# Moving one SBUF tile, and all tiles below it, down by 32 bytes in a two-layer encoder trunk

## The chip, the cores and the metric

The kernel runs on one core of a Trainium2 chip. The metric is the device time of one execution in microseconds (us); less is better. The core has a matrix engine (TensorE, PE in the profile, with its weight loads listed as PEld), VectorE (DVE), ScalarE (ACT), GpSimd (POOL), a queue engine (SyncE, SP) that issues most transfers, and 16 DMA engines. SBUF is the on-chip memory: 128 partitions, and a tile has the same byte address in each of them. PSUM holds the sums of TensorE.

## The reference

Two layers work on 512 tokens of 1024 features. In each layer:

```
proj = h @ w_in[l]                       # 1024 -> 1536, cut into q, k, v of two head groups
oa = global attention, ob = windowed attention, both normed per head
h = layer_norm(ALPHA * h + concat(oa, ob) @ w_o[l])
q = (h @ wq)                             # 8 heads x 2 halves x 128
pick, per token and head, the 16 best of 128 x 128 experts; g = softmax of their scores
a = gelu(u[e] . h) for each picked expert e;   w = g * a
h = layer_norm(ALPHA * h + sum_e w[e] * v[e])
```

The expert tables `u` and `v` have 16384 rows of 1024 float32 each per layer. This last part takes most of the time.

## The kernel before

**Two ways to the experts.** The 512 tokens are four chunks of 128. Chunk 0 (`gat`) gathers the rows of its picked experts by indirect DMA and works on VectorE. Chunks 1 to 3 (`dense`, `ND` = 384 tokens) multiply with all experts on TensorE, 128 experts (a block) at a time, and the gates that are zero drop what isn't wanted. There are `NB` = 128 blocks per layer.

**Splitting float32.** Every large product is made of three products of reduced operands (`F32R`): an operand x is cast to a high part on ScalarE, and VectorE subtracts to get the low part; then hi·hi, hi·lo and lo·hi are summed in PSUM.

**First expert product** (`acts`, lines 850 to 852). For a block, `ut` (the turned expert rows) is loaded, split into `uh` and `ul`, and for each of 8 slices of the features TensorE runs

```
pe.matmul(b[:, :ND], uh[:, k, :], xTh[:, k, :], ...)
pe.matmul(b[:, :ND], uh[:, k, :], xTl[:, k, :], ...)
pe.matmul(b[:, :ND], ul[:, k, :], xTh[:, k, :], ...)
```

The first operand is stationary (its 128 columns are loaded as weights), the second is the moving one (384 columns stream through). So a group of this product is 24 matmuls, and there are 256 groups. `xTh` and `xTl` are the two halves of the tile `xT`, the turned tokens.

**Second expert product** (`combine`, lines 1044 to 1046). `vt` is split into `vh` and `vl`, the weighted activations `w` into `wh` and `wl`, and for three chunks and two halves of the features the three products go into six PSUM banks. `wh` and `wl` are stationary, `vh` and `vl` moving with 512 columns. A group is 18 matmuls; there are 256 groups.

**Order on TensorE.** In each layer 24 groups of the first product (`LEAD`) are made ahead, in part between the small products of `spread` that build the gates (lines 917 and 918); then 104 times a group of the first product stands before a group of the second; and 24 groups of the second come last. In those last ones (`turn`) the operands take turns: tiles of the pool `ep`, then pieces of the tile `xT`, then the places of `uh`, `ul` and `ge`.

**Where tiles lie.** Pools open on the left side (addresses from below) or on the right (from the top down). On the right `xq` opens first; it has one place of 24576 bytes per partition, which `hTl` (low part of the tokens for the projections), then `oTp` (attention output of the first two chunks), then `xT` use in turn. Below it lie `kp` and `tp` (ranking of the keys), later `sp` (`o12`, `ah`, `al`, half of the `stg`) and then `ep` (`vh`, `vl`, `w`, `wh`, `wl`, the accumulators of the gather). All other operands of the products (`hTh`, `whi`, `wlo`, `wqh`, `wql`, `woh`, `wol`, `uh`, `ul`, the `ge` places, and `ut`, `vt`, `gg`) lie on the left.

Other products of this kind with 256 moving columns: the projections (lines 280 to 282; `hTh`/`hTl` stationary, the split weights moving), the queries of the key ranking (lines 547 to 549; split weights stationary, `xT` moving) and the attention output (lines 448 to 450; `oTp` stationary, split weights moving).

Of the kernel before, what the change touches and what calls it, by code (L numbers as in the profile page):

```python
# [9 lines left out]
F32R = mybir.dt.float32r  # L10
# [8 lines left out]
P = 128  # L19
D = 1024  # L20
KD = D // P
S = 512
# [14 lines left out]
GB = 4  # L37
LEAD = 24
REST = 3
NTAIL = 6  # L40
NCAND = [TK // (a + 1) for a in range(TK)]
COFF = [sum(NCAND[:a]) for a in range(TK)]
# [4 lines left out]
def encoder_kernel(ctx: ExitStack, tc: tile.TileContext, x, ln_in_g, ln_in_b, w_in, qn_g, kn_g, sink,  # L47
# [9 lines left out]
    ND = len(dense) * P  # L57
# [8 lines left out]
    def sbuf(name, bufs=1, side="left"):  # L66
        return tc.alloc_tile_pool(name=name, bufs=bufs, side=side, reuse_waits="tile")
# [55 lines left out]
    def transpose_rows(src, dst, nm, lo=None, gain=None, halves=(0, 1)):  # L123

        for q in halves:
            qs = slice(q * 4, (q + 1) * 4)
            b = acc_bank(nm)
            for i in range(4):
                k = q * 4 + i
                pe.transpose(b[:, i * P:(i + 1) * P], src[:, k * P:(k + 1) * P], ident)  # L130
            bv = b.rearrange("p (k t) -> p k t", k=4)
            if gain is not None:
                v.tensor_tensor(out=dst[:, qs, :], in0=bv, in1=bc(gain[:, qs, None], [P, 4, P]), op=MUL)
            else:
                act.copy(dst[:, qs, :], bv)
            if lo is not None:
                v.tensor_tensor(out=lo[:, qs, :], in0=bv, in1=dst[:, qs, :].bitcast(F32), op=SUB)
# [62 lines left out]
    for l in range(L):  # L200
        xq = sbuf(f"xq{l}", side="right")
# [55 lines left out]
        order = dense + gat  # L257
        pj = sbuf(f"pj{l}", bufs=2)
        hTh = pj.tile([P, KD, S], F32R, name="hTh", bufs=1)
        hTl = xq.tile([P, 2 * KD * ND], F32R, tag="x", name="hTl")[:, :KD * S].rearrange("p (k t) -> p k t", k=KD)  # L260
        def load_split(src, nm, w=None):

            w = load_w(src, nm) if w is None else w
            r = []
            for i in range(2):
                x_ = w[:, i * D:(i + 1) * D]
                hi = pj.tile([P, 4, 256], F32R, tag="whi", name="whi", bufs=4)
                lo = pj.tile([P, 4, 256], F32R, tag="wlo", name="wlo", bufs=4)
                act.copy(hi.rearrange("p k n -> p (k n)"), x_)
                v.tensor_tensor(out=lo.rearrange("p k n -> p (k n)"), in0=x_,  # L270
                                in1=hi.rearrange("p k n -> p (k n)").bitcast(F32), op=SUB)
                r.append((hi, lo))
            return r
# [196 lines left out]
        def flip_out(c, half):  # L470
            x_ = ao.tile([P, KD, P], F32, tag="oT", name="oT", bufs=1) if half == 0 else st[c]["oTx"]
            st[c]["oTx"] = x_
            if half == 0:
                st[c]["oT"] = x_, None
                if c in order[:2]:
                    if c == order[0]:
                        t = xq.tile([P, 2 * KD * ND], F32R, tag="x", name="oTp")
                        st["pair"] = t[:, :KD * S].rearrange("p (i k t) -> p i k t", i=2, k=KD)
                    ci = order.index(c)
                    st[c]["oT"] = tuple(st["pair"][:, i, :, ci * P:(ci + 1) * P] for i in range(2))  # L480
            transpose_rows(st[c]["o"].rearrange("p n d -> p (n d)"), x_, f"tr_o{c}", gain=gn, halves=(half,))
            hi, lo = st[c]["oT"]
            if lo is not None:
                qs = slice(half * 4, half * 4 + 4)
                act.copy(hi[:, qs, :], x_[:, qs, :])
                v.tensor_tensor(out=lo[:, qs, :], in0=x_[:, qs, :], in1=hi[:, qs, :].bitcast(F32), op=SUB)
# [190 lines left out]
        def flip_x(g, ci, half):  # L677
            if (ci, half) == (0, 0):
                if g == 0:
                    t = xq.tile([P, 2, KD, ND], F32R, tag="x", name="xT")  # L680
                    xTs["d"] = t[:, 0], t[:, 1]
                    xTs[g] = t[:, 0, :, :2 * P], t[:, 1, :, :2 * P]
                else:
                    pl, tag = (ac, "q") if g == 1 else (pt, "xT")
                    xTs[g] = pl.tile([P, KD, P], F32, tag=tag, name=f"xT{g}", bufs=1), None
            c = groups[g][ci]
            hi, lo = (t if t is None else t[:, :, ci * P:(ci + 1) * P] for t in xTs[g])
            transpose_rows(h[:, c, :], hi, f"tr_x{c}", lo=lo, halves=(half,))
            if (g, half) == (1, 1):
                hi_, lo_ = (t[:, :, 2 * P:] for t in xTs["d"])  # L690
                act.copy(hi_, hi)
                v.tensor_tensor(out=lo_, in0=hi, in1=hi_.bitcast(F32), op=SUB)
# [36 lines left out]
        for i in range(n + 3):  # L729
# [12 lines left out]
            if 0 <= i - 3 < n:  # L742
                c, hd = hs_[i - 3]
                values(c, hd, pTs.pop(i - 3))
                if hd == 15:
                    finish(c)
                    if c != order[3]:
                        at(i + 4, flip_out, c, 0)
                        at(i + 5, flip_out, c, 1)
                    if c == order[1]:  # L750
                        for j in range(4):
                            at(i + 6 + j, mix2, order[:2], j)
                        for u in range(2):
                            for half in range(2):
                                at(i + 9, norm_pair, order[u], half)
                        for u in range(2):
                            for half in range(2):
                                at(i + 12 + 2 * u + half, flip_x, 0, u, half)
                        at(i + 16, lambda: first.append(start(0)))
                        for u in range(16, 32):  # L760
                            if u % 4:
                                at(i + u, lambda: next(first[0]))
                    if c == order[2]:
                        for j in range(4):
                            at(i + 6 + j, mix2, [c], j)
                        at(i + 9, layer_norm, c, g_1, b_1)
                        for half in range(2):
                            at(i + 13 + half, flip_x, 1, 0, half)
# [8 lines left out]
        for half in range(2):  # L777
            flip_out(last, half)
# [8 lines left out]
        for half in range(2):  # L787
            flip_x(2, 0, half)
# [148 lines left out]
        for i, _ in enumerate(spread()):  # L937
            if i % 2 == 0 and len(gel) < LEAD - REST:
                next(am)
# [112 lines left out]
        with tc.manual_schedule(engines={mybir.EngineType.DVE}):  # L1052
            for g2 in range(NB // 2):
# [8 lines left out]
                for bi in range(2):  # L1062
# [4 lines left out]
                    if turn == 1:  # L1067
                        t = xTs["d"][blk // 3 % 2].rearrange("p k n -> p (k n)")
# [16 lines left out]
                    v.tensor_tensor(out=wl, in0=wf, in1=wh.bitcast(F32), op=SUB)  # L1085
                    if blk < NB - NTAIL:
                        for c in dense:
# [91 lines left out]
```

## Time and profile before

| | us |
|---|---|
| median of 3 runs (3043.37 to 3045.31) | 3043.95 |
| the profiled execution, its own time | 3047.03 |
| its span, first to last instruction | 3045.3 |
| TensorE busy | 2974.0 |
| VectorE busy | 2447.4 |
| ScalarE busy | 1318.1 |

The profiled execution is 3.1 us over the median, and 1.7 us of its time lie outside the span. Busy time of TensorE is the union of its matmuls; each is drawn from the start of its stream to the end of its drain, so neighbours overlap, and the distance from one start to the next is what a matmul takes of the span. The granted TensorE clock was 0.994 of full speed over the span.

### The profile page before, as it was taken

How to read it: one execution, taken by the hardware profiler on the slowest of the kernel's cores; microseconds unless marked ns; L12 is line 12 of the kernel's file. 1: busy time of each engine (PE TensorE's matmuls, PEld its weight loads, DVE VectorE, ACT ScalarE, POOL GpSimd, SP SyncE). 2: the span in 40 equal slices, each digit the busy share in tenths (PEclk: the TensorE clock that was granted, in tenths of full speed). 3: DMA queues.
4: the chain of work that ended last, by engine and by line, in shares of the span. 5: the costliest groups of instructions: out<-in, count | busy, mean ns of one | idle time of the engine just before them, and what ended most of it. 6: DMA issues, size and time to landing. Idle time of an engine off the chain costs nothing.

```text
span 3045.3 us, 48000 instructions
## 1 busy us (share of the span) xinstructions
PE 2974.0 (98%) x18034; PEld 2734.8 (90%) x18034; DVE 2447.4 (80%) x5084; ACT 1318.1 (43%) x2642; POOL 749.8 (25%) x524
## 2 busy tenths in 40 slices
PE   7999999999999999999999999999999999999998
PEld 7999899899999999998798998998999999999987
DVE  7777999778887887877777779997787788778877
ACT  4665167433333333333347641774333333333332
POOL 0000000014443455554000000000244444555530
PEclk9999999999999999999999999999999999999999
DMA  5014766669889989988420247666689998999882
GB/s 197 26 63 143 256 244 267 215 210 331 316 324 326 330 309 331 323 322 301 159 97 15 72 153 272 249 255 215 224 316 332 326 328 312 330 323 332 313 297 90
DMA packets 262233, 749.47 MB, mean 246 GB/s; under 512 B 19952, under 2 KB 130288, under 8 KB 231792
## 3 DMA queue, kind: packets, MB, share of 16 engines
q1 hardware_dynamic: 188272, 477.94, 43.8%
q0 software_dynamic: 73728, 268.47, 24.6%
q8 instruction: 141, 2.31, 0.3%
q14 instruction: 92, 0.75, 0.1%
HBM read 691.81 MB, written 54.53 MB: 245 GB/s over the span
## 4 chain that ended last, share of the span: by engine, by line
PE 72%; DVE 12%; issue 6%; DMA 5%; POOL 3%; ACT 2%; DVEq 0%; POOLq 0%; ACTq 0%
PE ps_a L850 10%; PE ps_a L852 10%; PE ps_a L851 10%; PE ff L1046 9%; PE ff L1045 9%; PE ff L1044 9%; DMA gt<-in_dram,idx 5%; POOL gt L1001 3%; PE ps_o L415 2%; PE ps_g L918 1%; PE ps_g L917 1%; PE ps_pt L401 1%; PE ps_s L377 1%; DVE ix L571 1%; PE ps_q L282 1%
## 5 line engine op out<-in xcount | busy, mean ns | idle before, releaser
L1001 POOL DMA_INDIRECT gt<-in_dram,idx x512 | 740.4, 1446 | 2014.8 <-DMA ut<-in_dram 1218.1
L850 PE MATMUL ps_a<-xT,uh 128*128 128x384 f32 x2048 | 697.1, 340 | 0.3
L852 PE MATMUL ps_a<-xT,ul 128*128 128x384 f32 x2048 | 695.9, 340 | 0.0
L851 PE MATMUL ps_a<-xT,uh 128*128 128x384 f32 x2048 | 694.9, 339 | 0.0
L1046 PE MATMUL ff<-vh,wl 128*128 128x512 f32 x1440 | 566.3, 393 | 0.0
L1045 PE MATMUL ff<-vl,wh 128*128 128x512 f32 x1440 | 564.3, 392 | 0.0
L1044 PE MATMUL ff<-vh,wh 128*128 128x512 f32 x1440 | 560.5, 389 | 2.1 <-ACT wh L1084 2.1
L1077 ACT CAST vh<-vt 128x1024 fp32r<-128x1024 f32 x240 | 251.7, 1050 | 561.3 <-PE ff L1046 290.0
L1078 DVE TENSOR_TENSOR vl<-vt,vh 128x1024 fp32r<-128x1024 f32 x240 | 293.8, 1224 | 132.7 <-ACT vh L1077 132.3
L851 PEld LDWEIGHTS ps_a<-xT,uh 128*128 128x128 f32 x2048 | 385.0, 188 | 9.6
L850 PEld LDWEIGHTS ps_a<-xT,uh 128*128 128x128 f32 x2048 | 385.0, 188 | 8.7 <-ACT ge L854 0.6
L852 PEld LDWEIGHTS ps_a<-xT,ul 128*128 128x128 f32 x2048 | 384.9, 188 | 0.0
L1018 DVE SCALAR_TENSOR_TENSOR gacc<-gt,gw,gacc 128x1024 f32<-128x1024 f32 x252 | 313.2, 1281 | 46.3 <-DMA gt<-in_dram,idx 45.9
L847 ACT CAST uh<-ut 128x1024 fp32r<-128x1024 f32 x256 | 269.8, 1054 | 178.7 <-PE ps_a L851 168.8
L1007 DVE CUSTOM_DVE_ANT_0 junk<-gt,h 128x1024 bf16<-128x1024 f32 x256 | 313.1, 1223 | 34.8 <-DMA gt<-in_dram,idx 30.1
L848 DVE TENSOR_TENSOR ul<-ut,uh 128x1024 fp32r<-128x1024 f32 x256 | 312.3, 1220 | 21.1 <-ACT uh L847 14.4
L1084 ACT CAST wh<-w 128x384 fp32r<-128x384 f32 x240 | 123.3, 514 | 468.3 <-DVE w L1081 468.1
L1046 PEld LDWEIGHTS ff<-vh,wl 128*128 128x128 f32 x1440 | 270.2, 188 | 57.2
L1044 PEld LDWEIGHTS ff<-vh,wh 128*128 128x128 f32 x1440 | 270.6, 188 | 54.7 <-ACT wh L1084 2.8
L1045 PEld LDWEIGHTS ff<-vl,wh 128*128 128x128 f32 x1440 | 270.2, 188 | 52.9
L1085 DVE TENSOR_TENSOR wl<-w,wh 128x384 fp32r<-128x384 f32 x240 | 134.0, 558 | 154.1 <-ACT wh L1084 154.1
L1081 DVE SCALAR_TENSOR_TENSOR w<-gg,ge 128x384 f32<-128x384 f32 x256 | 141.8, 554 | 6.2 <-DMA gg<-G 6.2
(278 smaller groups left out, 4630.1 us busy)
## 6 DMA issues: line engine op xcount, KB each, us to landing
ut<-in_dram SPq DMA_DIRECT2D x128, 1024.0 KB, 8.9
vt<-in_dram SPq DMA_DIRECT2D x128, 1024.0 KB, 7.6
w_pq<-in_dram SPq DMA_DIRECT2D x48, 1024.0 KB, 5.1
gg<-G SPq DMA_DIRECT2D x62, 768.0 KB, 15.0
G<-stg SPq DMA_DIRECT2D x24, 1920.0 KB, 6.3
w_o<-in_dram SPq DMA_DIRECT2D x24, 1024.0 KB, 4.9
w_q<-in_dram SPq DMA_DIRECT2D x8, 1024.0 KB, 5.4
gt<-in_dram,idx POOLq DMA_INDIRECT x512, 7.6
```

The source lines that it names most:

```text
L847: act.copy(uh.rearrange(ff), us)
L848: v.tensor_tensor(out=ul.rearrange(ff), in0=us, in1=uh.rearrange(ff).bitcast(F32), op=SUB)
L850: pe.matmul(b[:, :ND], uh[:, k, :], xTh[:, k, :], start=k == 0, stop=False)
L851: pe.matmul(b[:, :ND], uh[:, k, :], xTl[:, k, :], start=False, stop=False)
L852: pe.matmul(b[:, :ND], ul[:, k, :], xTh[:, k, :], start=False, stop=k == KD - 1)
L1001: pool.indirect_dma_start(out=t, out_offset=None, in_=src, in_offset=bass.IndirectOffsetOnAxis(ap=idx[:, j:j + 1], axis=0))
L1007: v.tensor_tensor_reduce(out=jk, in0=t, in1=h[:, c, :], op0=MUL, op1=ADD, scale=1.0, scalar=0.0, accum_out=a_[:, j:j + 1])
L1018: v.scalar_tensor_tensor(acc[j % 2], t, w_[:, j:j + 1], acc[j % 2], op0=MUL, op1=ADD)
L1044: pe.matmul(b, wh[:, cs], vh[:, ns], start=blk == 0, stop=False)
L1045: pe.matmul(b, wh[:, cs], vl[:, ns], start=False, stop=False)
L1046: pe.matmul(b, wl[:, cs], vh[:, ns], start=False, stop=blk == NB - 1)
L1078: v.tensor_tensor(out=vl, in0=vt[:, bi, :], in1=vh.bitcast(F32), op=SUB)
```

## The change

A constant `PAD` = 8 is added, and the three tiles that use the place in `xq` are asked for with 8 more float32 elements. The elements added are not used. The place grows from 24576 to 24608 bytes per partition, and as it hangs from the top of SBUF, it begins 32 bytes lower, and so does each tile of the right side below it. Nothing on the left moves.

```diff
+PAD = 8
...
-        hTl = xq.tile([P, 2 * KD * ND], F32R, tag="x", name="hTl")[:, :KD * S].rearrange("p (k t) -> p k t", k=KD)
+        hTl = xq.tile([P, 2 * KD * ND + PAD], F32R, tag="x", name="hTl")[:, :KD * S].rearrange("p (k t) -> p k t", k=KD)
...
-                        t = xq.tile([P, 2 * KD * ND], F32R, tag="x", name="oTp")
+                        t = xq.tile([P, 2 * KD * ND + PAD], F32R, tag="x", name="oTp")
...
-                    t = xq.tile([P, 2, KD, ND], F32R, tag="x", name="xT")
+                    t = xq.tile([P, 2 * KD * ND + PAD], F32R, tag="x", name="xT")[:, :2 * KD * ND].rearrange("p (i k t) -> p i k t", i=2, k=KD)
```

Addresses of the built programs, as the remainder modulo 256 (the slices of an operand that the matmuls take begin at multiples of 512 bytes in its tile, and share its remainder):

| operands | before | after |
|---|---|---|
| `uh`, `ul`, `ge` places, `hTh`, `whi`, `wlo`, `wqh`, `wql`, `woh`, `wol`, `qT`, `khh`, `kll`, `ut`, `vt`, `gg` | 192 | 192 |
| `xT`, `oTp`, `hTl` | 224 | 192 |
| `vh`, `vl`, `wh`, `wl`, `w` in `ep` | 224 | 192 |
| `keys`, `pq`, `psc`, `o12`, `ah`, `al`, the `stg` in `sp` | 224 | 192 |

In the built programs the instructions of every engine and every queue are the same in kind, shape, names and order; their line numbers are one higher, as the new constant takes a line.

## Rows read from the trace of the kernel before

**Rows 1.** The page's first part: busy us (share of the span) xinstructions.

```profile
PE 2974.0 (98%) x18034; PEld 2734.8 (90%) x18034; DVE 2447.4 (80%) x5084; ACT 1318.1 (43%) x2642; POOL 749.8 (25%) x524
```

**Rows 2.** Busy time in two stretches of 150 us, one of each layer's expert products.

```profile
core 0: us, PE busy (x) PEld busy (x) DVE busy (x) ACT busy (x) POOL busy (x), PEclk, DMA share, GB/s
...
900.00:1050.00 150.00, 150.00 (x754) 136.49 (x753) 120.70 (x172) 53.54 (x72) 63.21 (x50) 1.00 0.91 323
...
2550.00:2700.00 150.00, 150.00 (x754) 136.63 (x753) 120.56 (x129) 54.18 (x73) 76.36 (x50) 1.00 0.90 322
```

**Rows 3.** Waits of ScalarE: us in total, times, longest us.

```profile
ACT vh L1077 <- PE ff L1046: 290.0, 110, 2.9
```

**Rows 4.** Groups of TensorE by shape: busy us, mean ns of one.

```profile
L850 PE MATMUL ps_a<-xT,uh 128*128 128x384 f32 x2048 | 697.1, 340 | 0.3
L852 PE MATMUL ps_a<-xT,ul 128*128 128x384 f32 x2048 | 695.9, 340 | 0.0
L851 PE MATMUL ps_a<-xT,uh 128*128 128x384 f32 x2048 | 694.9, 339 | 0.0
L1046 PE MATMUL ff<-vh,wl 128*128 128x512 f32 x1440 | 566.3, 393 | 0.0
L1045 PE MATMUL ff<-vl,wh 128*128 128x512 f32 x1440 | 564.3, 392 | 0.0
L1044 PE MATMUL ff<-vh,wh 128*128 128x512 f32 x1440 | 560.5, 389 | 2.1 <-ACT wh L1084 2.1
...
L377 PE MATMUL ps_s<-kll,qT 128*128 128x384 f32 x32 | 10.8, 338 | 0.0
```

**Rows 5.** Timeline, TensorE, one group of each expert product: start us, us.

```profile
1001.21 0.39 PE L1044 MATMUL ff<-vh,wh 128*128 128x512 f32 x1
...
1003.29 0.39 PE L1044 MATMUL ff<-vh,wh 128*128 128x512 f32 x1
...
1005.11 0.40 PE L1046 MATMUL ff<-vh,wl 128*128 128x512 f32 x1
1005.34 0.34 PE L850 MATMUL ps_a<-xT,uh 128*128 128x384 f32 x1
...
1009.40 0.34 PE L852 MATMUL ps_a<-xT,ul 128*128 128x384 f32 x1
1009.58 0.39 PE L1044 MATMUL ff<-vh,wh 128*128 128x512 f32 x1
```

**Rows 6.** Timeline, TensorE, a late group whose operands lie in the tile xT.

```profile
1428.08 0.39 PE L1044 MATMUL ff<-xT 128*128 128x512 f32 x1
...
1431.93 0.40 PE L1046 MATMUL ff<-xT 128*128 128x512 f32 x1
1432.17 0.39 PE L1044 MATMUL ff<-vh,wh 128*128 128x512 f32 x1
```

**Rows 7.** Timeline, TensorE, two early groups of the first expert product, among spread's.

```profile
503.87 0.33 PE L851 MATMUL ps_a<-xT,uh 128*128 128x384 f32 x1
...
507.68 0.34 PE L852 MATMUL ps_a<-xT,ul 128*128 128x384 f32 x1
...
509.94 0.34 PE L851 MATMUL ps_a<-xT,uh 128*128 128x384 f32 x1
...
513.83 0.34 PE L852 MATMUL ps_a<-xT,ul 128*128 128x384 f32 x1
```

**Rows 8.** Timeline, TensorE, products of 256 columns: projections, then queries of the keys.

```profile
86.09 0.28 PE L280 MATMUL ps_q<-whi,hTh 128*128 128x256 f32 x1
...
91.77 0.28 PE L280 MATMUL ps_q<-whi,hTh 128*128 128x256 f32 x1
...
1812.92 0.28 PE L547 MATMUL ps_pq<-xT,wqh 128*128 128x256 f32 x1
...
1815.02 0.28 PE L547 MATMUL ps_pq<-xT,wqh 128*128 128x256 f32 x1
```

**Rows 9.** Groups of VectorE: the same subtraction into left tiles and into right ones.

```profile
L848 DVE TENSOR_TENSOR ul<-ut,uh 128x1024 fp32r<-128x1024 f32 x256 | 312.3, 1220 | 21.1 <-ACT uh L847 14.4 <-PE ps_g L918 6.7
L1078 DVE TENSOR_TENSOR vl<-vt,vh 128x1024 fp32r<-128x1024 f32 x240 | 293.8, 1224 | 132.7 <-ACT vh L1077 132.3
```

## The prediction, made before the changed kernel ran

> **What bounds the kernel.** The page's busy times come first: TensorE is busy for 2974.0 of 3045.3 us, VectorE for four fifths [rows 1]. A share over the span says little, so the next view is the busy time by stretches. In both layers' expert products TensorE is busy for 150.00 of 150.00 us at a granted clock of 1.00 (of 2.4 GHz), VectorE for 121 us, and the DMA engines are at 0.91 and 0.90 [rows 2]. Who waits for whom agrees: ScalarE stood 290.0 us before the cast into `vh` until TensorE let go of the buffer [rows 3]. So in this stretch, which is over half the span, every nanosecond between two matmul starts is in the end time, and the reader has to look at the distance of starts, not at the drawn durations, which overlap.
>
> The timeline gives that distance. A group of the second product takes 1001.21 to 1005.34, 4.13 us for 18 matmuls of 512 columns; one of the first product 1005.34 to 1009.58, 4.24 us for 24 matmuls of 384 [rows 5]. At 2.4 GHz, 512 columns are 213.3 ns and 384 are 160.0 ns. The means are 229.4 and 176.7 ns. So each matmul loses 16 to 17 ns to something, some 8% of the stretch, and only that can answer to a change of addresses.
>
> **Does an offset matter at all?** While one matmul streams, the weights of the next are read from the same memory. Call a step *equal* where the moving operand and the next weights have the same remainder modulo 256, else *unequal*. Before, the second product is equal inside (224 and 224, or 192 and 192 in its last turns), the first is unequal (`xT` 224, `uh` and `ul` 192). Three readings speak for an influence.
>
> First, inside a group of the second product the distance isn't constant. The first nine take 1001.21 to 1003.29, 231 ns each; the next eight 1003.29 to 1005.11, 227.5 ns each [rows 5]. It settles. In the late group with operands in `xT` it is settled from the start: 1428.08 to 1431.93, 17 steps of 226.5 ns [rows 6]. The last step of that group, the only one to weights at 192, is 0.24 us [rows 6]; and the step from the second to the first product, unequal too, is 0.23 (1005.11 to 1005.34) [rows 5]. So an unequal step appears to throw the pattern out, and it takes nine equal steps to settle again.
>
> Second, the first product, unequal at every step, has two patterns. Two early groups 6 us apart: 503.87 to 507.68 is 22 steps of 173.2 ns, 509.94 to 513.83 is 22 steps of 176.8 ns [rows 7]; the groups of the long stretch are of the second kind (176.7). 173.2 is the settled 226.5 of the second product less 53.3 for 128 columns. A loss of 13.2 ns is thus what settled matmuls show at either width.
>
> Third, the one equal product of 384 columns, the window scores, has a mean duration of 338 ns where the first expert product has 340, 340 and 339 [rows 4]; its 32 instances stand alone between transposes, so they show a size and not a settled state.
>
> **The change, part by part.** Instructions, their order, waits and transfers stay. What changes:
>
> *First expert product, now equal.* I take it that the settled loss holds at 384 columns too: 24 steps of 173.2 instead of 176.7 ns, 84 ns a group. 208 groups stand between groups of the second product: 17.5 us. Of the 48 early ones half are already settled by the look of [rows 7]; the other 24 give 24 x 84 ns = 2.0 us. Bounds: nothing (the pattern stays at 176.7), or, below, a loss that vanishes altogether, 24 x 16.7 ns x 256 = 103 us, for which no row speaks, since equal steps lose 13.2.
>
> *Second expert product, equal before and after.* What changes is its neighbours: with no unequal step on either side nothing throws it out, and 18 x 226.5 = 4.08 us replaces 4.13: 53 ns, times 208, 11.0 us. The 48 late groups are nearly settled: 1428.08 to 1432.17 is 4.09 [rows 6]; 0.5 us for all. Bounds: 0 and 11.5 us.
>
> *Products of 256 columns.* Here equal may be the worse state. The settled loss of 13.2 ns would make 106.7 into 119.9 ns. The queries of the keys, unequal before, take 1812.92 to 1815.02, 18 steps of 116.7 ns; the projections, unequal in one step of three, 86.09 to 91.77, 48 steps of 118.3 [rows 8]. 768 x 3.2 + 1152 x 1.6 and 384 x 1.6 for the attention output: 2.5 + 1.8 + 0.6 = 4.9 us lost. TensorE isn't without gaps there, so this is the upper bound; the lower is nothing. I take it whole.
>
> *VectorE, ScalarE and transfers.* The same subtraction takes 1220 ns into a left tile (192) and 1224 ns into a right one (224) [rows 9]. 4 ns x 240 is 1 us of an engine that has a fifth of its time free: nothing. If TensorE's stretch gets 1.5% shorter, the DMA share goes from 0.91 to 0.92 [rows 2]: still not the bound, and VectorE at 121 of 148 us neither.
>
> Sum: -17.5 - 2.0 - 11.0 - 0.5 + 4.9 = -26.1 us. The profiled execution had 3047.03 us; it would have 3020.9. Against the median, 3.1 us lower, the forecast is 3043.95 - 26.1 = 3018 us.
>
> [...]
>
> **The rivals.**
> 1. *Nothing moves.* The patterns are set by how a group begins (clocks, the queue of loads), not by remainders; the two early groups of [rows 7] have the same remainders and differ, which speaks for it. Then 3044 us, with at most 5 us for the 256-column products. [...] Against it: the steps that differ in remainder are the ones that throw the pattern out [rows 5, 6].
> 2. *Half of it.* Equal steps of 384 columns don't settle, but lose as the window scores do: 338 against a mean of 339.7 ns [rows 4], 1.7 ns x 6144 = 10 us; the second product stays thrown out by them. 3043.95 - 10 + 5 = 3039, or 3034 without the 256-column loss.
> 3. *Slower.* [...] The one equal step of 384 columns in the stretch, into the second product, takes 0.18 us (1009.40 to 1009.58) [rows 5]. Were all of them 180 ns: 3.3 x 6144 = 20 us more, with 5 us at 256 columns 3069 us. It decides against the change as soon as the mean step of the first product is over 176.7 + 1 ns, if the second keeps its 4.13 us. Against it: at 512 columns equal steps of 231 to 240 ns occur but don't last.
> 4. *Far faster*: the loss vanishes. Over 60 us less; no row has it.
>
> **How the numbers follow.** The settled state gets 0.48, range 3012 (no loss at 256 columns) to 3026 (the second product keeps half its loss); half of it 0.16; nothing 0.15; slower 0.18; far faster 0.03. Faster by over 0.2% (6 us, about what the runs can tell from no change: they lie within 2 us) takes the settled, far faster, and all but 0.02 of the half case: 0.65. Nothing and that remainder: 0.17. Slower: 0.18. The range leaves out the far gain and the worse part of the slower case: 3008 to 3054.
>
> **What would show it.** Right: a group of 24 at 4.16 us and one of 18 at 4.08, with no slow first nine; the group means of lines 850 to 852 (one line lower after) at 336 ns and those of the second product all at 389; the queries of the keys at 119 to 120 ns a step. TensorE still at 150 of 150. Wrong: 24 groups still at 4.24 (rival 1), distances that wander between 174 and 182 (rival 2), or a constant step over 177 (rival 3). The step most likely to fail is the one from 512 columns to 384: that the settled loss is the same there.

## The result, and the profile after

| | us, median | lowest to highest | runs |
|---|---|---|---|
| before | 3044.63 | 3043.37 to 3046.99 | 4 |
| changed | 3029.08 | 3025.03 to 3029.56 | 4 |

The ratio is 0.9945, with a 95% interval of 0.9928 to 0.9962: the change makes the kernel 0.4 to 0.7% faster. The profiled execution of the changed kernel took 3028.79 us, with a span of 3027.0 (3045.3 before). The line numbers of the changed kernel are one higher: L851 to L853 are the first expert product, L1045 to L1047 the second.

The page's first part for the changed kernel (busy us, share of the span, instructions), and its busy time in the same two stretches of 150 us as [rows 2]:

```profile
PE 2960.1 (98%) x18034; PEld 2725.8 (90%) x18034; DVE 2447.3 (81%) x5084; ACT 1317.9 (44%) x2642; POOL 742.0 (25%) x524
```

```profile
900.00:1050.00 150.00, 150.00 (x759) 136.58 (x759) 120.89 (x174) 54.58 (x75) 67.71 (x51) 1.00 0.90 328
2550.00:2700.00 150.00, 150.00 (x759) 136.57 (x759) 121.09 (x125) 54.56 (x74) 75.62 (x50) 1.00 0.92 330
```

TensorE is busy for 150.00 of 150.00 us still, at the same granted clock of 1.00, but it now gets through 759 matmuls in a stretch where it was 754. VectorE stays at 121 us, and the DMA engines are at 0.90 and 0.92.

TensorE's groups by shape in the changed kernel (busy us, mean ns of one; compare [rows 4]):

```profile
L851 PE MATMUL ps_a<-xT,uh 128*128 128x384 f32 x2048 | 692.5, 338 | 0.3
L853 PE MATMUL ps_a<-xT,ul 128*128 128x384 f32 x2048 | 690.6, 337 | 0.0
L852 PE MATMUL ps_a<-xT,uh 128*128 128x384 f32 x2048 | 689.2, 337 | 0.0
L1047 PE MATMUL ff<-vh,wl 128*128 128x512 f32 x1440 | 564.9, 392 | 0.0
L1046 PE MATMUL ff<-vl,wh 128*128 128x512 f32 x1440 | 564.4, 392 | 0.0
L1045 PE MATMUL ff<-vh,wh 128*128 128x512 f32 x1440 | 560.6, 389 | 0.0
```

The first product fell from 340, 340 and 339 ns to 338, 337 and 337, the second hardly at all. The drawn durations overlap, so the distances of starts have to say how much that is. TensorE's timeline in the changed kernel, one group of the second product and one of the first (start us, us):

```profile
998.58 0.39 PE L1045 MATMUL ff<-vh,wh 128*128 128x512 f32 x1
...
1000.66 0.39 PE L1045 MATMUL ff<-vh,wh 128*128 128x512 f32 x1
...
1002.47 0.39 PE L1047 MATMUL ff<-vh,wl 128*128 128x512 f32 x1
1002.70 0.33 PE L851 MATMUL ps_a<-xT,uh 128*128 128x384 f32 x1
...
1003.77 0.33 PE L851 MATMUL ps_a<-xT,uh 128*128 128x384 f32 x1
...
1006.89 0.39 PE L1045 MATMUL ff<-vh,wh 128*128 128x512 f32 x1
```

The second product: its first nine matmuls take 998.58 to 1000.66, 2.08 us or 231 ns each, the other nine 1000.66 to 1002.70, 226.7 ns each. The slow first nine of [rows 5] are still there. The first product: the first six take 1002.70 to 1003.77, 178 ns each, the other eighteen 1003.77 to 1006.89, 173.3 ns each; before, all 24 went at 176.7. So the settled pattern has come to 384 columns, with a slow beginning of its own. A group of each is 4.12 and 4.19 us, where it was 4.13 and 4.24.

A late group with operands in `xT`, in the changed kernel's timeline (answers to [rows 6]):

```profile
1422.11 0.39 PE L1045 MATMUL ff<-xT 128*128 128x512 f32 x1
...
1425.97 0.39 PE L1047 MATMUL ff<-xT 128*128 128x512 f32 x1
1426.19 0.39 PE L1045 MATMUL ff<-vh,wh 128*128 128x512 f32 x1
```

Seventeen steps take 3.86 us, 227 ns each, and the step to the next tile 0.22: the 0.24 of [rows 6] is gone.

Products of 256 columns in the changed kernel's timeline, projections and queries of the keys (answer to [rows 8]; each line stands for one matmul of three):

```profile
86.14 0.28 PE L281 MATMUL ps_q<-whi,hTh 128*128 128x256 f32 x1
...
88.66 0.28 PE L281 MATMUL ps_q<-whi,hTh 128*128 128x256 f32 x1
...
1802.30 0.28 PE L548 MATMUL ps_pq<-xT,wqh 128*128 128x256 f32 x1
...
1805.54 0.28 PE L548 MATMUL ps_pq<-xT,wqh 128*128 128x256 f32 x1
```

86.14 to 88.66 are 21 steps of 120.0 ns (118.3 before), 1802.30 to 1805.54 are 27 steps of 120.0 ns (116.7 before).

Where the time came from is read from the first and last start of the expert products' matmuls in each layer. First the kernel before, layer by layer (count: lowest/median/highest ns of one, first and last start in us):

```profile
L850 PE MATMUL ps_a<-xT,uh x1024: 332/338/522, 397.5 to 1419.3; 128*128 128x384 f32 x171
...
L1044 PE MATMUL ff<-vh,wh x720: 387/389/499, 557.4 to 1524.9; 128*128 128x512 f32 x180
...
L850 PE MATMUL ps_a<-xT,uh x1024: 331/338/688, 1910.2 to 2932.1; 128*128 128x384 f32 x171
...
L1044 PE MATMUL ff<-vh,wh x720: 387/389/499, 2070.2 to 3035.1; 128*128 128x512 f32 x180
```

The changed kernel, the same groups:

```profile
L851 PE MATMUL ps_a<-xT,uh x1024: 331/334/523, 398.6 to 1413.4; 128*128 128x384 f32 x171
...
L1045 PE MATMUL ff<-vh,wh x720: 386/389/498, 558.3 to 1515.6; 128*128 128x512 f32 x180
...
L851 PE MATMUL ps_a<-xT,uh x1024: 332/334/526, 1899.9 to 2914.6; 128*128 128x384 f32 x171
...
L1045 PE MATMUL ff<-vh,wh x720: 387/389/504, 2059.5 to 3016.8; 128*128 128x512 f32 x180
```

From the first matmul of the first product to the last of the second, the first layer takes 1127.4 us before (397.5 to 1524.9) and 1117.0 after (398.6 to 1515.6); the second 1124.9 (1910.2 to 3035.1) and 1116.9 (1899.9 to 3016.8). That is 10.4 and 8.0, 18.4 us of the span's 18.3. In the first layer's 10.4 stands one wait. In its last turns, TensorE waited for `wh` in the profiled execution of the kernel before (start us, us; in brackets the idle time before and who ended it):

```profile
1501.39 0.49 PE L1046 MATMUL ff<-xT 128*128 128x512 f32 x1
1504.02 0.50 PE L1044 MATMUL ff<-vh,wh 128*128 128x512 f32 x1 [2.13 <-ACT wh L1084]
```

The step is 2.63 us long. Nothing of the kind is in its second layer or in the changed kernel, but three of the kernels below have a wait at this line as well, of 1.0 to 1.9 us. So I count it to that execution and not to the change; about 16 us of the 18.4 are then the change's. What lies ahead of and between these stages takes 0.1 us more: 397.5 and 385.3 us before, 398.6 and 384.3 after.

### The profile page after: what moved, and what is told of

The parts are those of the page before. It is cut to its first block, busy times and chain, and to the rows that moved or that the text cites. A ratio compares the mean times of both kernels' runs of the same rounds, so it can differ in the third digit from the quotient of the medians.

```text
span 3027.0 us, 48000 instructions
## 1 busy us (share of the span) xinstructions
PE 2960.1 (98%) x18034; PEld 2725.8 (90%) x18034; DVE 2447.3 (81%) x5084; ACT 1317.9 (44%) x2642; POOL 742.0 (25%) x524
## 4 chain that ended last, share of the span: by engine, by line
PE 87%; DVE 10%; ACT 1%; issue 1%; DMA 0%; SPq 0%; DVEq 0%; ACTq 0%
PE ps_a L851 12%; PE ps_a L853 12%; PE ps_a L852 12%; PE ff L1046 12%; PE ff L1047 12%; PE ff L1045 12%; PE ps_o L416 2%; PE ps_g L919 1%; PE ps_g L918 1%; PE ps_pq L546 1%; PE ps_pt L402 1%; PE ps_s L378 1%; DVE ix L572 1%; DVE sv L570 1%; DVE wql L510 1%
## 5 line engine op out<-in xcount | busy, mean ns | idle before, releaser
L1002 POOL DMA_INDIRECT gt<-in_dram,idx x512 | 732.7, 1431 | 2004.0 <-DMA ut<-in_dram 608.0
L851 PE MATMUL ps_a<-xT,uh 128*128 128x384 f32 x2048 | 692.5, 338 | 0.3
L853 PE MATMUL ps_a<-xT,ul 128*128 128x384 f32 x2048 | 690.6, 337 | 0.0
L1047 PE MATMUL ff<-vh,wl 128*128 128x512 f32 x1440 | 564.9, 392 | 0.0
L1045 PE MATMUL ff<-vh,wh 128*128 128x512 f32 x1440 | 560.6, 389 | 0.0
L851 PEld LDWEIGHTS ps_a<-xT,uh 128*128 128x128 f32 x2048 | 386.0, 188 | 8.7 <-ACT ge L855 0.6
L1079 DVE TENSOR_TENSOR vl<-vt,vh 128x1024 fp32r<-128x1024 f32 x240 | 293.7, 1224 | 118.4 <-ACT vh L1078 117.8
L853 PEld LDWEIGHTS ps_a<-xT,ul 128*128 128x128 f32 x2048 | 385.4, 188 | 0.0
L1008 DVE CUSTOM_DVE_ANT_0 junk<-gt,h 128x1024 bf16<-128x1024 f32 x256 | 313.2, 1223 | 41.0 <-DMA gt<-in_dram,idx 36.7
L1019 DVE SCALAR_TENSOR_TENSOR gacc<-gt,gw,gacc 128x1024 f32<-128x1024 f32 x252 | 313.8, 1280 | 35.9 <-DMA gt<-in_dram,idx 35.4
L1047 PEld LDWEIGHTS ff<-vh,wl 128*128 128x128 f32 x1440 | 270.3, 188 | 56.7
L1045 PEld LDWEIGHTS ff<-vh,wh 128*128 128x128 f32 x1440 | 270.8, 188 | 52.3 <-ACT wh L1085 0.9
```

The source lines that it names most:

```text
L851: pe.matmul(b[:, :ND], uh[:, k, :], xTh[:, k, :], start=k == 0, stop=False)
L853: pe.matmul(b[:, :ND], ul[:, k, :], xTh[:, k, :], start=False, stop=k == KD - 1)
L1002: pool.indirect_dma_start(out=t, out_offset=None, in_=src, in_offset=bass.IndirectOffsetOnAxis(ap=idx[:, j:j + 1], axis=0))
L1008: v.tensor_tensor_reduce(out=jk, in0=t, in1=h[:, c, :], op0=MUL, op1=ADD, scale=1.0, scalar=0.0, accum_out=a_[:, j:j + 1])
L1019: v.scalar_tensor_tensor(acc[j % 2], t, w_[:, j:j + 1], acc[j % 2], op0=MUL, op1=ADD)
L1045: pe.matmul(b, wh[:, cs], vh[:, ns], start=blk == 0, stop=False)
```

## The experiments

All kernels but the last issue the same instructions in the same order as the kernel before, and differ in addresses alone. Their line numbers are those of the kernel before. *D* is from here on the address of the moving operand less that of the next weights, modulo 256: 0 for an equal step, +32 within the first product of the kernel before. The address of `xT` is set by a pad on the place in `xq` (which also sets the tiles below it) and by a slice that begins XO elements into the tile. To make room where the pad is large, the scratch tile `fx` of the key ranking is replaced by another scratch tile that is free there.

**Is it the equality, or the addresses themselves?** The kernel before, with a small unused tile that moves `uh` and `ul` to 224. The moving operand and the weights of the first product share a remainder again, now 224, and nothing else that the long stretch uses moves.

```diff
-        up = sbuf(f"u{l}", bufs=2)
+        up = sbuf(f"u{l}", bufs=2); up.tile([P, 8], F32, tag="gap", name="gap", bufs=1)
```

> The kernel before, with uh and ul moved up by 32 bytes to the remainder 224, where xT already is; nothing else that the long stretch uses moves, except that the last turns find vh in the places of uh at 224 and wh at 192. Theory (equal remainders of the moving operand and the next weights let the steps settle): a group of 24 of the first product takes 4.18 to 4.19 us as in the changed kernel, the products of 256 columns stay as before, total 3024 to 3027 us. Rival 1 (the tiles now start at a multiple of 64 bytes, which 192 is and 224 isn't): groups stay at 4.24, total 3044 us. Rival 2 (the other moved tiles of the right side made the gain): 4.24, 3044 us.

Measured: 3029.26 us (3028.53 to 3030.44; before on the same chip 3043.25), ratio 0.9953 [0.9936, 0.9969]. The steps of both products are those of the changed kernel (table below). So what counts is the relation of the two addresses, and not that tiles lie at a multiple of 64 bytes; nor is it the many other tiles that the change moved. The time is 2 us over the range expected. In the last turns `vh` at 224 meets weights at 192 here, and those groups take 4.200 us, where the changed kernel's take 4.080. The projections and queries kept their old addresses and steps; what their 3 ns a step are worth can't be read from this total, as the last turns work against it.

**Is it `xT` alone?** The changed kernel, with `xT` moved back to 224 by a slice, and the rest of the right side left at 192.

```diff
-xT = xq.tile([P, 2 * KD * ND + PAD], ...)[:, :2 * KD * ND]...
+xT = xq.tile([P, 2 * KD * ND + PAD], ...)[:, 8:8 + 2 * KD * ND]...
```

> The changed kernel, with xT alone put back to the remainder 224 (it begins 32 bytes into its place); hTl, oTp and all tiles below stay at 192. Theory: the first product is unequal again, 4.24 us a group, the queries of the keys are back at 116.7 ns a step, the projections stay at 120: total 3044 to 3047 us. Rival 2 (the other moved tiles made the gain): stays near 3029 us.

Measured: 3033.25 us (3030.31 to 3039.01, 8 runs), ratio 0.9969 [0.9958, 0.998]: a miss, 11 us under what was expected. TensorE's timeline of this kernel, a group of the second product and one of the first:

```profile
990.42 0.39 PE L1044 MATMUL ff<-vh,wh 128*128 128x512 f32 x1
...
992.47 0.39 PE L1044 MATMUL ff<-vh,wh 128*128 128x512 f32 x1
...
994.50 0.34 PE L850 MATMUL ps_a<-xT,uh 128*128 128x384 f32 x1
...
995.57 0.34 PE L850 MATMUL ps_a<-xT,uh 128*128 128x384 f32 x1
...
998.75 0.39 PE L1044 MATMUL ff<-vh,wh 128*128 128x512 f32 x1
```

In the long stretch the first product went back as it should: 994.50 to 998.75 is 4.25 us, six steps 1.07 and no faster ones behind them. But the second, whose addresses are those of the changed kernel, is settled from its first step: 990.42 to 992.47 is 2.05 us for nine, 227.8 ns, and the whole group 4.08. What differs at its edges is the switch from the first product: the last matmul of the first product streams from 224 while the first weights of the second come from 192. An unequal step at the switch removed the slow beginning. The prediction held that such a step causes it.

**Both at once.** If so, a kernel with equal steps within both products and unequal ones at both switches should do without either slow beginning. `xT` at 192, as `uh` and `ul`; the second product's operands at 224.

```diff
-REST = 3
+REST = 3; PAD, XO, HO, OO = 64, 56, 0, 0
...
-xT = xq.tile([P, 2, KD, ND], ...)
+xT = xq.tile([P, 2 * KD * ND + PAD], ...)[:, XO:XO + 2 * KD * ND]...
```

> xT alone at 192; hTl, oTp and all tiles below it at 224 as in the kernel before (the place is 256 bytes longer; the scratch tile fx of the gather's ranks lies in ga to make room). Theory: the first product settles, 4.18 to 4.19 us a group; the steps between the two products are unequal and cost 8 ns each, 416 of them, 3 us; the projections are as before, 118.3 ns: total 3028 to 3032 us. Rival 2: 4.24 us a group, 3044 us.

Measured: 3020.43 us (3016.31 to 3023.91), ratio 0.9923 [0.9907, 0.994], 8 us under what was expected and a miss as well: the expectation still held that the unequal switches cost. Its timeline:

```profile
996.01 0.39 PE L1044 MATMUL ff<-vh,wh 128*128 128x512 f32 x1
...
998.05 0.39 PE L1044 MATMUL ff<-vh,wh 128*128 128x512 f32 x1
...
1000.10 0.34 PE L850 MATMUL ps_a<-xT,uh 128*128 128x384 f32 x1
...
1001.14 0.33 PE L850 MATMUL ps_a<-xT,uh 128*128 128x384 f32 x1
...
1004.26 0.39 PE L1044 MATMUL ff<-vh,wh 128*128 128x512 f32 x1
```

The first nine of the second product take 2.04 us (226.7 ns each), the group 4.09; the first six of the first product 1.04 (173.3 each), the group 4.16. Both run settled from the start.

**Does it need equality?** The same edit with other pads and slices, which put `xT` at other distances. Two ran four times each, `xT` at 64 (PAD 72, XO 32, which puts the tiles below at 192) and the tiles below at 160 (PAD 80, XO 8, with `hTl` and `oTp` kept at 224 by slices of 16 elements):

> The changed kernel with xT 128 bytes higher (remainder 64 against 192 of uh and ul; place 288 bytes longer, fx in ga). Theory in its first form (equal modulo 256 is what counts): unequal, 4.24 us a group, 3044 us. Theory with a period of 128 bytes: settles as in the changed kernel, 4.18 us, 3029 us. [...]

> xT, uh and ul at 192 and the tiles below xT at 160 (the place 320 bytes longer, hTl and oTp at 224). Both switches between the products are unequal as with xT alone, with the other sign. Theory A (an unequal switch of either sign lets both products settle at once): groups of 4.16 and 4.09 us, 3020 us. Theory B (the switch needs a given shift, and the sign counts: 32 bytes up into the first product, any into the second): the second product settled at 4.09, the first thrown out at 4.18 or more, 3025 to 3030 us.

Measured: 3030.62 us (3028.91 to 3032.73), ratio 0.9957 [0.994, 0.9973] for the first, and 3023.1 (3022.83 to 3024.01), ratio 0.9932 [0.9916, 0.9949] for the second. Four more were profiled once each, all with PAD 64, and XO of 8, 60, 48 and 16:

> xT at 0 (64 bytes above uh and ul modulo 256), the tiles below at 224. It asks how the loss goes with the distance: 0 gave 173.3 ns a step, 32 gave 176.7 and 128 gave 175.5. Theory (equal is the best): between 175 and 178 ns, a group of 24 at 4.20 to 4.27 us. [...]

> xT at 208, 16 bytes above uh and ul; the tiles below it at 224. The curve so far: 0 and 64 bytes settle at 173.3 ns a step, 32 at 176.7, 128 at 175.5. Theory (multiples of 64 below 128 settle): 16 doesn't, a step of 174 to 178 ns, a group of 24 at 4.18 to 4.27 us. Rival (only the last 32-byte piece counts, 16 is as good as 0): 173.3 ns, 4.16 us.

> xT at 160, 32 bytes below uh and ul; the tiles below it at 224. Theory (the distance counts whatever its sign): as 32 above, 176.7 ns a step, 4.24 us a group. Rival (the sign counts, as the products of 256 columns showed: 116.7 ns with the moving operand 32 above the weights, 118.2 with 32 below): another value, between 174 and 180 ns.

> xT at 32, 96 bytes above uh and ul modulo 256; the tiles below it at 224. Theory (odd multiples of 32 don't settle): 175 to 178 ns a step, 4.2 to 4.27 us a group. Rival (what counts is being within 64 bytes above; past it every distance is as 128): 175.5 ns, 4.21 us. A step under 173 ns would be a better place than any so far.

Measured: 3022.66, 3037.68, 3023.39 and 3040.86 us, one run each (before: 3044.36 beside the first, 3044.26 beside the others). The table holds all of these kernels. Steps are medians over the 206 groups of each product that alternate in the long stretches, worked out from the starts in the trace; "then" is the step that holds to the end of the group. The last two columns are the time against before on the same chip, and what the groups alone would make of it: 206 x (4.244 + 4.129 - the two group times).

| kernel | D in first | its first steps, ns | then | group us | D at switch to second | its first steps, ns | group us | measured us | by groups |
|---|---|---|---|---|---|---|---|---|---|
| before | +32 | 178 174 178 175 180 | the same, mean 176.7 | 4.244 | 0 | 229 233 236 224 231 236 228 233 231 | 4.129 | | |
| changed | 0 | 171 175 178 185 176 182 | 173.3 | 4.186 | 0 | 229 233 236 224 231 236 228 233 231 | 4.121 | -15.6 | -13.6 |
| `uh`, `ul` at 224 | 0 | 171 175 178 185 176 182 | 173.3 | 4.186 | 0 | as changed | 4.121 | -14.0 | -13.6 |
| `xT` back | +32 | as before | as before | 4.241 | +32 | 226 | 4.079 | -10.0 | -10.9 |
| `xT` alone | 0 | 174 174 175 | 173.3 | 4.163 | -32 | 228 | 4.090 | -22.8 | -24.7 |
| below at 160 | 0 | 174 176 182 | 173.3 | 4.173 | +32 | 226 | 4.087 | -21.3 | -23.3 |
| `xT` at 160 | -32 | 178 175 174 175 | 173.3 | 4.173 | -64 | 228 233 231 | 4.100 | -20.9 | -20.6 |
| `xT` at 0 | +64 | 169 176 | 173.3 | 4.165 | +32 | 226 236 228 233 231 | 4.108 | -21.7 | -20.6 |
| `xT` at 64 | +128 | 178 172 175 | the same, mean 175.6 | 4.212 | +128 | 235 233 | 4.095 | -12.6 | -13.6 |
| `xT` at 208 | +16 | 176 178 173 | the same, mean 175.7 | 4.218 | -16 | 226 236 228 232 231 | 4.108 | -6.6 | -9.7 |
| `xT` at 32 | +96 | 170 176 174 180 175 177 | the same, mean 176.5 | 4.223 | +64 | 230 231 236 228 233 231 | 4.117 | -3.4 | -6.8 |

The timeline of the kernel with `xT` at 160, one group of the first product, stands for an unequal one that settles:

```profile
1000.97 0.34 PE L850 MATMUL ps_a<-xT,uh 128*128 128x384 f32 x1
...
1002.01 0.34 PE L850 MATMUL ps_a<-xT,uh 128*128 128x384 f32 x1
...
1005.14 0.39 PE L1044 MATMUL ff<-vh,wh 128*128 128x512 f32 x1
```

1002.01 to 1005.14 is 3.13 us for 18 steps, 173.9 ns with the last one, into the second product (178); the mean of those between is 173.3.

Of the expectations, those for `xT` at 208 and at 32 came as their theory had them. `xT` at 0 and at 160 settled at 173.3 ns, where 175 to 178 were expected for the first, and 176.7 or another value between 174 and 180 for the second: both missed. `xT` at 64 took about the time that a period of 128 bytes would give (3029 us), but not by its steps: the first product stays at 175.6 ns, and the short beginning of the second makes up for it. With the tiles below at 160 both products come near theory A (4.16 and 4.09 us).

Three things follow. The steps account for the end time, kernel by kernel, within 4 us. Equality isn't the condition: in the long stretch distances of 0, +64 and -32 settle at 173.3 ns, those of +16, +32, +96 and +128 stay at 175.6 to 176.7. Nor does the distance alone decide: at +32 some groups among spread's do run at 173.2 to 173.4 ns, 12 of 26 in the kernel before (4.254 us a group, the others 4.324) and all 26 in the kernel with `xT` back, so that how a group begins counts too. And in the second product, whose steps settle at 227 in all of these kernels, the slow beginnings are mostly ends of one and the same run of steps, 229 233 236 224 231 236 228 233 231, entered at a later place.

**Do the queries' steps cost anything?** The kernel with `xT` alone, with the split key weights `wqh` and `wql` moved to 160, so that their distance is +32 again.

```diff
-                hi = kq.tile([P, KD, P], F32R, tag="wqh", name="wqh")
+                hi = kq.tile([P, D + 64], F32R, tag="wqh", name="wqh")[:, 56:56 + D].rearrange("p (k e) -> p k e", k=KD)
```

> xT alone at 192 as in the run before last, and the split weights of the key queries (wqh, wql) at 160, so that xT lies 32 bytes above them as it did at first (the place in kq is 256 bytes longer). Theory: the queries go back from 120 to 116.7 ns a step, the expert groups stay at 4.156 and 4.095 us: 2.5 us less than with xT alone, 3016 to 3020 us. Rival (32 bytes above only counts at the old place, or the queries are hidden): the same 3020 us as with xT alone.

Measured: 3019.43 us (3018.44 to 3024.95), ratio 0.9918 [0.9902, 0.9935]. Its timeline, queries of the keys:

```profile
1802.13 0.28 PE L547 MATMUL ps_pq<-xT,wqh 128*128 128x256 f32 x1
...
1805.28 0.28 PE L547 MATMUL ps_pq<-xT,wqh 128*128 128x256 f32 x1
```

27 steps in 3.15 us are 116.7 ns: the step came back as expected. The time is 1 us under the kernel without it, less than the runs of either spread. Its median is the lowest of the study, and it beats both the kernel before and the changed one, but what shows clear of the spread is the move of `xT` alone.

**What starts the slow beginning?** The changed kernel, with two groups of the first product ahead of two of the second, so that every other group follows one of its own column count. This one does change the order of the work.

```diff
-        while len(gel) < LEAD:
+        while len(gel) < LEAD - 2:
...
-                for bi in range(2):
-                    blk = g2 * 2 + bi
-                    if len(gel) < NB:
-                        next(am)
+                for _ in range(2):
+                    if len(gel) < NB:
+                        next(am)
+                for bi in range(2):
+                    blk = g2 * 2 + bi
```

> The changed kernel, with two groups of the first product and then two of the second (22 groups of the first made ahead instead of 24). Theory (the slow first steps belong to the switch of 384 to 512 columns and back, equal remainders or not): the second group of each pair has no slow steps, 4.16 and 4.08 us; 104 x 2 switches less at 0.025 and 0.041 us give 7 us, 3022 us. Rival (they belong to the beginning of every group, to its PSUM bank or its new tiles): all groups stay at 4.185 and 4.122, 3029 us. If the splitting on VectorE falls behind with this order, TensorE shows idle time in the stretch.

Measured: 3068.39 us (3063.94 to 3071.78), ratio 1.0084 [1.0067, 1.0101]: slower, a miss of the total. Its timeline, the second group of a pair of the second product, the pair of the first, and the next beginning of the second:

```profile
993.24 0.39 PE L1044 MATMUL ff<-vh,wh 128*128 128x512 f32 x1
...
997.32 0.33 PE L850 MATMUL ps_a<-xT,uh 128*128 128x384 f32 x1
...
998.39 0.33 PE L850 MATMUL ps_a<-xT,uh 128*128 128x384 f32 x1
...
1001.51 0.33 PE L850 MATMUL ps_a<-xT,uh 128*128 128x384 f32 x1
...
1005.67 0.39 PE L1044 MATMUL ff<-vh,wh 128*128 128x512 f32 x1
...
1007.75 0.39 PE L1044 MATMUL ff<-vh,wh 128*128 128x512 f32 x1
```

993.24 to 997.32 is a group of the second product that follows its like: 4.08 us, no slow step. The first product begins slowly, 998.39 - 997.32 = 1.07 for six, and its first group takes 4.19 (to 1001.51); the second, at the same addresses, takes 4.16 (to 1005.67), 173.3 a step. Then the second product begins slowly again, 2.08 us for nine. All steps are equal here, so the slow beginning comes with the switch between the products alone, as the theory had it. Whether the column count or something else that changes at the switch brings it, no run separates. Half of the slow beginnings were saved, yet the kernel got slower. Four of its waits, and then two of the same in the changed kernel (us in total, times, longest us):

```profile
DVE gacc L1018 <- DMA gt<-in_dram,idx: 109.0, 48, 5.5
...
DVE junk L1007 <- DMA gt<-in_dram,idx: 83.8, 36, 4.2
...
PE ps_a L852 <- DVE ul L848: 23.4, 13, 3.1
...
PE ff L1044 <- ACT wh L1085: 8.5, 4, 3.2
```

```profile
DVE junk L1008 <- DMA gt<-in_dram,idx: 36.7, 42, 2.8
DVE gacc L1019 <- DMA gt<-in_dram,idx: 35.4, 38, 2.8
```

VectorE stood longer for the gathered rows (109.0 and 83.8 us where it was 35.4 and 36.7), and TensorE stood 23.4 us for `ul` and 8.5 us for `wh`, neither of which is among the changed kernel's waits. Behind three of the longest of these waits ten matmuls each of the first product went at 320 ns, where 173.3 is the settled step, at a granted clock of 0.50: some 4 us more. That the late gathers made `ul` late is how I read these rows; no run took them apart.

## Why the prediction was right, and where it was not

**The bound** was as read: with no instruction moved, the end time followed the distance of starts in the two expert stages, 18.4 of 18.3 us, of which 2.6 are the one wait of the execution before.

**The loss of 16 to 17 ns a matmul** is counted at 2.4 GHz; the views give the granted clock as a share only. As a rate of columns, the trace of the kernel before bears the figure out, in a stretch and on a timeline at a granted clock of 0.50:

```profile
547.00:550.30 3.30, 3.30 (x21) 3.30 (x20) 0.25 (x1) 2.40 (x4) 0.00 (x0) 0.50 1.04 386
```

```profile
548.67 0.52 PE L852 MATMUL ps_a<-xT,ul 128*128 128x384 f32 x1
...
550.27 0.38 PE L851 MATMUL ps_a<-xT,uh 128*128 128x384 f32 x1
```

Five steps of 384 columns take 1.60 us, 320.0 ns each, and twelve of 256 columns (1796.27 to 1798.83, also at 0.50) 213.3 each: 1.2 columns a ns. Twice that at 1.00, an estimate from these steps, is 2.4 columns a ns, or 53.3 ns for 128, which is also what lies between the settled 173.2 and 226.5 ns [rows 6, 7].

**That an offset matters at all** holds. Moving `uh` and `ul` alone gave the whole of the change's effect, 14.0 us. A move by 32 bytes took a step from 176.7 to 173.3 ns; settled steps of 512 columns stayed at 226.7 ns in the long stretch. The next weights are loaded while a matmul streams, as the prediction has it: PEld is busy for 136.49 of 150.00 us without a gap on TensorE [rows 2], and for 136.58 in the changed kernel. That the two reads hold each other up is not shown by this. The word *equal* was too narrow, though: -32 and +64 settle too, and +32 in some of the early groups.

**The first product, -17.5 us:** that equal steps settle was right, and the step named as the likeliest to fail, the one from 512 columns to 384, held to the digit: 173.3 ns forecast 173.2. The size was off. The first six steps are slow (171 to 185), which takes 26 ns of the 84 a group back: 58 ns x 206 = 12.0 us. The 2.0 for the early groups is 1.0: 14 of the groups among spread's went from 4.324 to 4.254 us (medians, with a first step of 0.26 us), the others were settled before.

**The second product, -11.0 us:** this is the step that failed, "an unequal step appears to throw the pattern out". Its slow first nine are there with all steps equal, 4.121 us a group for 4.129: 8 ns x 206 = 1.7 us, all of it in the last step, no longer unequal (235 to 227). The rows that the step rested on showed two things together: in [rows 5] the slow beginning stands behind unequal steps and also behind a switch from the first product (384 columns) to the second (512); in [rows 6] neither is there. The pairs tell them apart: the switch is enough, with every step equal, for six or nine slow steps. In the kernels of the table an unequal step at the switch to the second product shortened its beginning or did away with it. Only within a product does the sentence hold: among the late groups of the kernel before, those behind an unequal step begin with a run of five or seven steps before they settle (4.113 and 4.106 us, medians), and in the changed kernel none does (4.080). So in the long stretch the edit kept what it was to remove.

**The 256-column products, +4.9 us:** the steps came as forecast, 120.0 from 116.7 and 118.3. Their price can't be told from nothing: outside the expert stages the changed kernel takes 0.1 us more, while the kernel with `uh` and `ul` at 224, whose products of 256 columns lie as in the kernel before, takes 2 us less than that one. TensorE isn't the bound there (365.99 busy of the first 397.5 us before), and the lower of the two bounds, nothing, was the nearer one.

**Sum:** forecast 26.1 us for the profiled execution; the groups give 12.0 + 1.0 + 1.7 and about 1.4 for the late groups (0.5 forecast), 16.1 us. The span fell by 18.3, with the wait of 2.6 in it, and the medians by 15.6. Forecast for the expert products alone were 31.0 (26.1, and the 4.9 that don't show), about twice what came: that the sum lies nearer is luck, as a loss that wasn't paid stood against a gain that was too large. What is missing of the gain is mostly the slow beginnings, (26 + 42 ns) x 206 = 14 us, and without them, in the kernel with `xT` alone, 22.8 us were measured. The time of 3029.08 lies nearer to the 3034 of the second rival than to 3018, but what that rival said, equal steps of 384 columns that don't settle, is not what happened. The first rival is out as it stands, as patterns do follow addresses, but it was right that the way a group begins counts too; the third is out, as the settled step isn't a long one.

What stays open is by what mechanism the addresses act, and what sets the place at which the run of slow steps is entered. The distance at the switch alone doesn't: +32 at the switch to the second product gave no slow step in two kernels, and five in the one with `xT` at 0.

## What to carry to other kernels

Where TensorE is busy without gaps, look at the distance of matmul starts, not at the drawn durations. Here the addresses of moving operand and next weights were worth some 3 ns a settled matmul at 256 and 384 columns, 7 at 512, and up to 12 in the first steps, and a few bytes of padding try that out without a change to the order of the work. Try several distances, here from -32 to +128 bytes, and look at the first steps after every switch between products as well as at the settled ones; here -32 at one switch and +32 at the other, with equal operands inside, gave 0.8% where equality everywhere gave 0.5%. When two conditions occur together in every row that a reading rests on, it is only half a reading: look for a place in the program where one stands alone, or build it.

## What the runs showed of the hardware that was not expected

- With equal addresses a settled matmul lost the same at all three widths: 120.0, 173.3 and 226.7 ns for 256, 384 and 512 columns, which at 2.4 columns a ns (the estimate above) would take 106.7, 160.0 and 213.3: 13.3 or 13.4 ns each. At a granted clock of 0.50 nothing of that showed: 256 columns took 213.3 ns and 384 took 320.0, in proportion, and those 320.0 came at a distance of +32 (the kernel before, above) as at 0 (the changed kernel, 2050.27 to 2053.15 us, nine steps).
- At 256 columns the settled step is not the best: 116.7 ns at a distance of +32 and of +16, 117.8 at +64, 118.3 at -32, 118.7 at +128, and 120.0 at +96 and 0 (queries of the keys, medians over stretches of 24 steps). At 384 columns the order is another one (table above), and at 512 columns a distance of +32 within a group gave 233 ns (the late groups of the kernel with `uh` and `ul` at 224, 4.200 us).
- The sign counts: at 384 columns -32 settled at 173.3 ns, and +32 stayed at 176.7 throughout the long stretch.
- An unequal step at the switch from 384 to 512 columns can be worth more than it costs: the last step of the group rises from 227 to 235 ns, and the nine long first steps go, which took 2081 ns where settled ones take 2040.
